# The two k weight pieces: split and stored in the first chunk instead of the second

## The chip, the cores and the metric

The kernel runs on one core of a Trainium2 chip. The metric is the device time of one execution in microseconds (us); the time of a kernel is the median of its runs. Profiles show one execution each.

## The reference

The reference is a trunk of two layers over 2560 tokens of 1024 channels: a prompt of 2048 tokens and a sample of 512, which are independent of each other. The first layer is attention in windows, with grouped heads; the second is a Fourier mixing layer. All of the change lies in the first one:

```python
def attention_layer(x, g, w_in, w_out, sink, rel_bias):
    b, s, _ = x.shape
    h = rmsnorm(x, g)
    z = h @ w_in
    q = z[..., :ATTN_WIDTH].reshape(b, s, N_HEADS, HEAD_DIM)
    k = z[..., ATTN_WIDTH:ATTN_WIDTH + KV_WIDTH].reshape(b, s, N_KV_HEADS, HEAD_DIM)
    v = z[..., ATTN_WIDTH + KV_WIDTH:ATTN_WIDTH + 2 * KV_WIDTH].reshape(b, s, N_KV_HEADS, HEAD_DIM)
    gate = z[..., ATTN_WIDTH + 2 * KV_WIDTH:]
    o = banded_gqa_with_sink(q, k, v, rel_bias, sink)
    return x + (o * jax.nn.silu(gate)) @ w_out
```

There are 16 query heads and 4 key heads of 64 channels. Each block of 128 queries sees 384 keys; the scores get a bias by relative position and the softmax has a learned sink. Everything is in 32-bit floats.

## The kernel before

**Products.** Each matrix product is made of three matmuls in a reduced 32-bit format (`fp32r`): an operand is split into a high part (its rounding, by a copy) and a low part (the rest, by a subtraction), and `matmul3` (lines 91 to 93) adds high x high, high x low and low x high. A weight piece is a tile of 128 x 1024 numbers before the split and `[128, 2, 1024]` after it: 0.5 MB raw, 1 MB split.

**Chunks.** The attention layer works through five chunks of 512 tokens: first the sample, then the four quarters of the prompt. In each chunk `make_h` brings the transposed activations (`xk`, L177), POOL scales them by the inverse norm (L179), and ACT and DVE make the high and low part of h (L183, L184; L191, L192 for the halo of 128 tokens). `kv_proj` makes k and v (`kp`, `kh`, `vp`). Then a loop of 64 steps runs over 8 pairs of heads and 8 halves of query blocks: scores (`spt`, L401), the softmax (L413 to L429), its transposes (`pt`, L440 to L442) and the product with v (`av`, L454). Between these steps TensorE is filled with the projections of the next pair's q and gate (`qp`, `gp`) and, in the last pair, with the output projection (`op`, on the pieces `wo`). Statistics of the next chunk's tokens (`xs`, L147) are spread over the steps too. Elements of `b` (L378, L382, L383) are the bias and the sink of a head.

**Weight pieces.** `load_w(c, n, ...)` (L95 to L120) delivers piece n of 28: 8 and 9 are k's, 10 and 11 are v's, 0 to 7 q's, 12 to 19 the gate's, the others the output's. In the first chunk the raw piece is loaded (`w32`, L109), ACT copies the high part (L110), and the low part is made by POOL in four quarters of 256 columns (L115) or by DVE at once (L117). The split piece is then stored in a DRAM buffer `wsd` (L119), unless n is in `AGAIN = (0, 8, 9, 10, 11, 12)`, the pieces that are wanted in the first microseconds. In the second chunk the pieces of `AGAIN` are loaded raw and split once more (ACT L101, DVE L102), and stored then by POOL's queue (L103); all others are read from `wsd` (L106), as all 28 are in the later chunks.

**Buffers and order.** Split pieces live in a ring of 4 tiles (tag `w`); raw pieces in the first chunk take tiles of two rings, `stage[0]` (tag `uT`, 8 tiles) or `stage[1]` (tag `x`, 4 tiles, which the activations, their statistics and the raw pieces of the second chunk use also). Loads are issued by SP, the stores of split pieces by POOL. A scheduler orders the instructions of each engine by the program's order and their dependencies; `after(ins, anchor)` adds a dependency of order alone: `ins` is put behind `anchor` and does not wait on its completion. `last_exp` holds the last exponential of the softmax that was issued.

Of the kernel before, what the change touches and what calls it, by code (L numbers as in the profile page):

```python
# [30 lines left out]
BIG = 1.0e30  # L31
LINE = 512
HALVES = ((1, 0), (1, 1), (0, 0), (0, 1))
AGAIN = (0, 8, 9, 10, 11, 12)
CH = 512
CHUNKS = [(2048, SEQ, T), (0, 0, SEQ), (512, 0, SEQ), (1024, 0, SEQ), (1536, 0, SEQ)]

# [1 line left out]
def f32(ap):  # L39
    return ap.bitcast(F32)  # L40
# [3 lines left out]
def encoder(  # L44
# [3 lines left out]
    PE, ACT, DVE, POOL, SP = nc.tensor, nc.scalar, nc.vector, nc.gpsimd, nc.sync  # L48
# [28 lines left out]
    def xtile(shape, dtype, name):  # L77
        return xp.tile(shape, dtype, align_bytes=LINE, tag="x", bufs=4, name=name)
# [13 lines left out]
        PE.matmul(out, a[0], b[1], start=False, stop=False, skip_group_check=more)  # L92
        PE.matmul(out, a[1], b[0], start=False, stop=stop, skip_group_check=more)  # L93

    def load_w(c, n, name, lo_engine=None):  # L95

        w = wp.tile([P, 2, D], F32R, align_bytes=LINE, tag="w", bufs=4, name=f"w{name}")
        if c == 1 and n in AGAIN:
            w32 = xtile([P, D], F32, f"w32{name}")
            SP.dma_start(w32, w_in[n])  # L100
            ACT.copy(w[:, 0], w32)  # L101
            DVE.tensor_tensor(w[:, 1], w32, f32(w[:, 0]), ALU.subtract)  # L102
            POOL.dma_start(f32(wsd[n]), f32(w))  # L103
            return w[:, 0], w[:, 1]
        if c:
            SP.dma_start(f32(w), f32(wsd[n]))  # L106
            return w[:, 0], w[:, 1]
        w32 = stage[n > 19 or n in (6, 7, 18, 19)](f"w32{name}")
        SP.dma_start(w32, w_in[n] if n < 20 else w_out[(n - 20) // 4, (n - 20) % 4])  # L109
        ACT.copy(w[:, 0], w32)  # L110
        if lo_engine is None:

            for i in range(4):
                cs = slice(i * 256, i * 256 + 256)
                POOL.tensor_tensor(w[:, 1, cs], w32[:, cs], f32(w[:, 0, cs]), ALU.subtract)  # L115
        else:
            lo_engine.tensor_tensor(w[:, 1], w32, f32(w[:, 0]), ALU.subtract)  # L117
        if n not in AGAIN:
            (SP if lo_engine else POOL).dma_start(f32(wsd[n]), f32(w))  # L119
        return w[:, 0], w[:, 1]  # L120

    stage, res_tile, ready = [], [], {}

    def after(ins, anchor):

        if anchor is not None:
            tc.add_manual_dep(ins.ins, anchor.ins.name, ISSUE, reason="issue order")

    def attention_phase():

        with ExitStack() as es:
# [6 lines left out]
            def stats(c):  # L138

                tok, lo_t, hi_t = CHUNKS[c]  # L140
                nt = min(640, hi_t - tok) // P
                ss = main.tile([P, 8], F32, tag="ss", bufs=2, name=f"ss{c}")

                def one(i):
                    xt = xtile([P, D], F32, f"xs{c}_{i}")
                    after(SP.dma_start(xt, x[tok + i * P : tok + (i + 1) * P, :]), last_exp[0])
                    sq = ACT.activation(xt, xt, AF.Square, accum_out=ss[:, i : i + 1])  # L147
                    after(sq, last_exp[0])

                return [lambda i=i: one(i) for i in range(nt)] + [lambda: inv_rms(ss, nt, f"inv{c}")]  # L150

            def spread(c, inv, place=None):

                tok, lo_t, hi_t = CHUNKS[c]
                nt = min(640, hi_t - tok) // P
                invb = ap.tile([P, 640], F32, tag="invb", name=f"invb{c}")
                for i0 in range(0, nt, 4):
                    m = min(4, nt - i0)
                    ps = bank(f"ib{c}_{i0}") if place is None else place
                    for i in range(m):  # L160
                        PE.transpose(ps[:, i * P : (i + 1) * P], inv[:, i0 + i : i0 + i + 1].to_broadcast([P, P]), ident)
                    ACT.copy(invb[:, i0 * P : (i0 + m) * P], ps[:, : m * P])  # L162
                return invb
# [40 lines left out]

            last_u = [None, None]
            early = [load_w(0, 8, "k0_0", DVE)]
            hs, halo = make_h(0, None)
            early.append(load_w(0, 9, "k0_1", DVE))

            def bias_rows():  # L210
# [27 lines left out]
            last_exp, last_evac, last_mul = [None], [None], [None]  # L238
# [7 lines left out]
            def kv_proj(c, hs, halo, norms=None, early=None):  # L246
# [9 lines left out]
                def evac_k(t, ps, n, wc):  # L256
                    ps = scaled(ps, invb, f"k{t}")
                    for j in range(2):
# [3 lines left out]
                        for rows in (slice(0, 64), slice(64, 128)):  # L262
                            ACT.copy(kw[rows, 0, cs], sp)
                            DVE.tensor_tensor(kw[rows, 1, cs], sp, f32(kw[rows, 0, cs]), ALU.subtract)

                wk = early or [load_w(c, 8 + t, f"k{c}_{t}", DVE) for t in range(2)]

                def wslice(w, k, c0, n):
# [352 lines left out]
            for c in range(len(CHUNKS)):  # L621

                if c > 1:
                    hs, halo = make_h(c, invb)
                for s in tail:
                    s()
                if c == 1:
                    hs, halo = make_h(c, invb)
                if c:
                    invb0 = kv_proj(c, hs, halo)  # L630
                else:
                    invb0 = kv_proj(c, hs, halo, first_norms, early)
                rowd, sk = bias
                uTs = []
                res = [{} for p in range(8)]
                at = [attention(c, p, res[p], uTs) for p in range(8)]
                for s in qg_proj(c, 0, hs, res[0], invb0):
                    s()
                at[0][0]()
                fill = []  # L640
                for i in range(64 + LAG + AVLAG):
                    p, n = divmod(i, 8)
                    if n == 0 and i < 64:
                        if p < 7:

                            fill = qg_proj(c, p + 1, hs, res[p + 1], invb0)
                            fill.pop(0)()
                            at[p + 1][0]()
                            if i == 0 and c == 0:

                                for s in fill[:8]:
                                    s()
                                fill = fill[8:]
                        else:
                            op = out_proj(c, uTs)
                            fill, rest, tail = op[:4], op[4:7], op[7:]
                    if c + 1 < len(CHUNKS):
                        if i == 24:
                            norm_steps = stats(c + 1)
                        if i >= 28 and i % 4 == 0 and norm_steps:  # L660
                            inv = norm_steps.pop(0)()
                        elif i == 56:
                            invb = spread(c + 1, inv)
                    if i in (4, 8, 12, 16) and c in EXTRA:
                        EXTRA[c].pop(0)()
                    if c == len(CHUNKS) - 1 and i in AHEAD:
                        AHEAD[i]()
                    if i < 64:
                        at[p][1](*HB[n])
                    k = i - LAG  # L670
                    if 0 <= k < 64:
                        at[k // 8][2](*HB[k % 8])
                    if i < 64:
                        m = len(fill) * (n + 1) // 8 - len(fill) * n // 8
                        todo = fill[len(fill) * n // 8 :][:m]
                        for s in todo[: m // 2]:
                            s()
                    k -= AVLAG
                    if 0 <= k < 64 and k % 2 == 1:
                        b = k % 8 // 2  # L680
                        at[k // 8][3](b)
                        if b % 2 == 1:
                            at[k // 8][4](b)
                    if i < 64:
                        for s in todo[m // 2 :]:
                            s()
                    elif rest:
                        rest.pop(0)()
            return tail

    def fourier_phase(tail):
        with ExitStack() as es:
# [522 lines left out]
            for i, f in enumerate(pend):  # L1215
                finish(*f, last=i == len(pend) - 1)

    fourier_phase(attention_phase())


# [96 lines left out]
```

## Time and profile before

| | |
|---|---|
| median of three runs | 1666.79 us (1666.54, 1669.78, 1666.79) |
| profiled execution | 1669.14 us |
| its span | 1667.3 us |
| mean granted TensorE clock | 0.997 |
| busy: TensorE, VectorE, ScalarE, GpSimd | 1641.9, 1173.9, 874.8, 377.7 us |
| data moved | 338.39 MB, mean 203 GB/s |

Engines are named PE (TensorE matmul), PEld (its weight loads), DVE (VectorE), ACT (ScalarE), POOL (GpSimd) and SP (SyncE); SPq and POOLq are the queues in which they issue transfers. `L101` is line 101 of the kernel. Times within a profile count from the start of its span; the execution takes 1.84 us more than its span. Of a matmul that overlaps the next one the profile models the end, so a row's length is longer than the distance to the next row. `PEclk` is the granted clock, 1.00 being full speed. What stands in brackets behind an instruction is the idle time of its engine before it and what ended it. In a row of a group, the tile left of the arrow is written and those right of it are read.

The first chunk takes from the start to about 230 us, where the second chunk's first matmul of k (`kp`) stands. The attention layer ends near 1117 us, where the Fourier layer follows.

### The profile page before, as it was taken

The page shows a single profiled execution, that of the slowest core. Times are in us where ns is not written, and L with a number is a line of the kernel's source. Part 1 is how long each engine was busy: PE and PEld are TensorE (multiplying, and loading weights), DVE is VectorE, ACT ScalarE, POOL GpSimd, SP SyncE. Part 2 cuts the span into 40 slices and gives each one's busy share as a digit, 9 for nine tenths or more (in the row PEclk, how much of TensorE's full clock was granted, in tenths as well). Part 3 has the DMA queues.
Part 4 walks back from the last instruction along what each step waited for, and adds up shares of the span by engine and source line. Part 5 has one row for each costly group of instructions (what it writes and reads, how often), then busy time and mean ns, then how long its engine had stood idle before and what let it go on. Part 6 is the DMA issues. An engine that isn't in the chain of part 4 may idle for free.

```text
span 1667.3 us, 25637 instructions
## 1 busy us (share of the span) xinstructions
PE 1641.9 (98%) x8987; PEld 1412.0 (85%) x8987; DVE 1173.9 (70%) x2812; ACT 874.8 (52%) x1998; POOL 377.7 (23%) x528
## 2 busy tenths in 40 slices
PE   9999999999999999999999999999999999999997
PEld 7888778888898888988888888888888887888886
DVE  6777665888538886478874588768576768888553
ACT  6788644676336764256652466546554545342321
POOL 2345641211403113121123211221111111111000
PEclk9999999999999999999999999999999999999999
DMA  8456886444765456754548644656456578453331
GB/s 296 167 216 224 291 318 226 181 175 175 276 222 182 158 183 211 263 200 150 199 142 327 229 166 152 231 202 246 165 196 234 183 249 316 167 187 125 113 127 51
DMA packets 89964, 338.39 MB, mean 203 GB/s; under 512 B 11067, under 2 KB 21307, under 8 KB 72684
## 3 DMA queue, kind: packets, MB, share of 16 engines
q1 hardware_dynamic: 71388, 259.40, 44.3%
q0 software_dynamic: 18160, 76.56, 11.7%
q8 instruction: 72, 1.18, 0.3%
q10 hardware_dynamic: 288, 0.79, 0.1%
q14 instruction: 56, 0.46, 0.1%
HBM read 261.18 MB, written 75.53 MB: 202 GB/s over the span
## 4 chain that ended last, share of the span: by engine, by line
PE 83%; DVE 5%; ACT 5%; DMA 4%; issue 2%; POOL 1%; SPq 0%; POOLq 0%; DVEq 0%; ACTq 0%
PE av L454 6%; PE spt L401 5%; PE pt L440 5%; PE qp L91 4%; PE qp L93 4%; PE qp L92 4%; PE gp L91 4%; PE gp L93 4%; PE gp L92 4%; PE op L91 3%; PE op L92 3%; PE op L93 3%; PE fo L92 3%; PE fo L93 3%; PE fo L91 3%; PE W L91 2%
## 5 line engine op out<-in xcount | busy, mean ns | idle before, releaser
L417 ACT ACTIVATE S<-S 128x385 f32<-128x385 f32 (+1 forms) x320 | 191.1, 597 | 44.6 <-DVE S L413 42.8
L441 ACT CAST pts<-pt 128x384 fp32r<-128x384 f32 (+1 forms) x320 | 144.2, 454 | 111.3 <-PE pt L440 106.9
L442 DVE TENSOR_TENSOR pts<-pt,pts 128x384 fp32r<-128x384 f32 (+1 forms) x320 | 168.5, 527 | 43.7 <-ACT pts L441 40.8
L413 DVE CUSTOM_DVE_ANT_0 S<-spt,b 128x385 f32<-128x385 f32 (+1 forms) x320 | 168.8, 528 | 34.6 <-PE spt L401 31.6
L401 PE MATMUL spt<-kwin,qab 128*128 128x384 f32 (+1 forms) x640 | 157.2, 327 | 1.1 <-DVE S L413 1.1
L473 POOL TENSOR_TENSOR o<-o,s 128x256 f32<-128x256 f32 x75 | 55.6, 741 | 445.0 <-DVE o L471 444.7
L440 PE MATMUL pt<-ident,S 128*128 128x128 f32 x896 | 150.6, 273 | 1.1 <-ACT S L426 0.9
L401 PEld LDWEIGHTS spt<-kwin,qab 128*128 128x128 f32 x640 | 118.2, 188 | 26.8 <-DVE S L413 1.7
L454 PEld LDWEIGHTS av<-pts,v 128*128 128x128 f32 x896 | 126.3, 189 | 14.8 <-DVE qab L350 1.6
L454 PE MATMUL av<-pts,v 128*128 128x256 f32 x896 | 136.3, 285 | 1.9 <-DVE qab L350 1.7
L91 PE MATMUL gp<-h,wg 128*128 128x512 f32 x320 | 137.8, 431 | 0.0
L91 PE MATMUL qp<-h,wq 128*128 128x512 f32 x320 | 136.8, 428 | 0.0
L91 PE MATMUL op<-wo,uT 128*128 128x512 f32 x320 | 126.5, 397 | 1.5 <-ACT invb L162 0.8
L440 PEld LDWEIGHTS pt<-ident,S 128*128 128x128 f32 x896 | 113.6, 140 | 16.0 <-DVE pts L442 3.2
L91 PE MATMUL fo<-wo,tTu 128*128 128x512 f32 x320 | 125.8, 393 | 1.3 <-ACT wo L1119 1.3
L93 PE MATMUL qp<-h,wq 128*128 128x512 f32 x320 | 126.1, 394 | 0.0
L93 PE MATMUL gp<-h,wg 128*128 128x512 f32 x320 | 125.9, 393 | 0.0
L92 PE MATMUL qp<-h,wq 128*128 128x512 f32 x320 | 125.8, 393 | 0.0
L92 PE MATMUL op<-wo,uT 128*128 128x512 f32 x320 | 125.7, 393 | 0.0
L92 PE MATMUL gp<-h,wg 128*128 128x512 f32 x320 | 125.7, 393 | 0.0
L92 PE MATMUL fo<-wo,tTu 128*128 128x512 f32 x320 | 125.4, 392 | 0.0
L93 PE MATMUL fo<-wo,tTu 128*128 128x512 f32 x320 | 124.7, 390 | 0.0
(356 smaller groups left out, 4090.2 us busy)
## 6 DMA issues: line engine op xcount, KB each, us to landing
wo<-wsd SPq DMA_DIRECT2D x32, 1024.0 KB, 5.0
wq<-wsd SPq DMA_DIRECT2D x31, 1024.0 KB, 4.8
wg<-wsd SPq DMA_DIRECT2D x31, 1024.0 KB, 6.2
x<-x1d SPq DMA_DIRECT2D x40, 512.0 KB, 3.3
b<-b21d SPq DMA_DIRECT2D x40, 512.0 KB, 5.6
b<-rowd SPq DMA_DIRECT2D x40, 384.0 KB, 4.2
xs<-in_x_dram SPq DMA_DIRECT2D x23, 512.0 KB, 6.5
s2d<-gt POOLq DMA_DIRECT2D x40, 256.0 KB, 3.5
```

The lines of the kernel that those rows point to most:

```text
L91: PE.matmul(out, a[0], b[0], start=start, stop=False, skip_group_check=more)
L92: PE.matmul(out, a[0], b[1], start=False, stop=False, skip_group_check=more)
L93: PE.matmul(out, a[1], b[0], start=False, stop=stop, skip_group_check=more)
L401: PE.matmul(ps[:, 2 + k0 * P : 2 + k1 * P], q, kwin[g][:, part, b * P + k0 * P : b * P + k1 * P], start=part == 0, stop=part == 1,)
L413: DVE.tensor_tensor_reduce(out=s[:, e0:e1], in0=ps[:, 1 + e0 : 1 + e1], in1=st["bias"][:, j, 386 - e1 : 386 - e0][:, ::-1], scale=1.0, sca ...
L417: last_exp[0] = ACT.activation(s[:, e0:e1], s[:, e0:e1], AF.Exp, bias=mn, scale=-1.0, accum_out=den)
L440: PE.transpose(ps[:, kb, :], s[:, 1 + kb * P : 1 + (kb + 1) * P], ident)
L441: ACT.copy(hi[:, k0:k1, j, :], ps[:, k0:k1, :])
L442: DVE.tensor_tensor(lo[:, k0:k1, j, :], ps[:, k0:k1, :], f32(hi[:, k0:k1, j, :]), ALU.subtract)
L454: PE.matmul(out, v, pt[:, kb].rearrange("p h q -> p (h q)"), start=kb == k0 and part == 0, stop=kb == k1 - 1 and part == 1,)
L473: eng.tensor_tensor(o, o, s, ALU.mult)
```

## The change

Pieces 8 and 9 leave `AGAIN` and form `LATE`. They are still split at the start of the first chunk as before, without a store. In the same chunk, at the fourth step of the second pair of heads (p = 1) and of the third pair (p = 2), `load_w` is called once more for one of them each: SP loads the raw piece into a tile of the `x` ring, ordered behind the last exponential; ACT copies the high part, POOL makes the low part in four quarters and stores the split piece. In the second chunk `load_w` then reads both from `wsd` as any other piece.

```diff
-AGAIN = (0, 8, 9, 10, 11, 12)
+LATE = (8, 9)
+AGAIN = (0, 10, 11, 12)
...
-    def load_w(c, n, name, lo_engine=None):
+    def load_w(c, n, name, lo_engine=None, late=None):
...
-        w32 = stage[n > 19 or n in (6, 7, 18, 19)](f"w32{name}")
-        SP.dma_start(w32, w_in[n] if n < 20 else w_out[(n - 20) // 4, (n - 20) % 4])
+        w32 = stage[late is not None or n > 19 or n in (6, 7, 18, 19)](f"w32{name}")
+        load = SP.dma_start(w32, w_in[n] if n < 20 else w_out[(n - 20) // 4, (n - 20) % 4])
+        if late:
+            after(load, late)
         ACT.copy(w[:, 0], w32)
...
-        if n not in AGAIN:
+        if late or n not in LATE + AGAIN:
             (SP if lo_engine else POOL).dma_start(f32(wsd[n]), f32(w))
         return w[:, 0], w[:, 1]
...
                     if c == len(CHUNKS) - 1 and i in AHEAD:
                         AHEAD[i]()
+                    if c == 0 and i % 8 == 3 and 1 <= p < 3:
+                        load_w(0, LATE[p - 1], f"late{p}", late=last_exp[0])
                     if i < 64:
                         at[p][1](*HB[n])
```

In the order of instructions that the scheduler makes of it, TensorE's is unchanged. On ACT, DVE, POOL and SP the order differs in the second to fourth pair of heads of the first chunk and at the start of the second chunk, and nowhere else.

## The prediction

> **What bounds the kernel now.** I read the slices of the page first, then a table of stretches, then TensorE's timeline where the change acts, then the chain of waits into it.
>
> ```profile
> PE   9999999999999999999999999999999999999997
> PEclk9999999999999999999999999999999999999999
> ```
>
> TensorE is busy nearly everywhere. So an edit can save only where TensorE stands idle, and costs only where it makes TensorE stand. The table (length, busy time and count of PE, PEld, DVE, ACT, POOL, then granted clock, DMA share, GB/s) says where that is:
>
> ```profile
> 55.00:110.00 55.00, 55.00 (x321) 48.12 (x320) 44.63 (x158) 45.35 (x113) 26.12 (x38) 1.00 0.48 175
> 110.00:180.00 70.00, 65.13 (x366) 54.80 (x365) 54.09 (x186) 59.21 (x147) 40.08 (x58) 1.00 0.70 262
> ...
> 229.00:238.00 9.00, 7.21 (x24) 5.15 (x23) 7.62 (x10) 5.09 (x6) 3.39 (x7) 0.81 0.90 320
> ...
> 262.00:1117.00 855.00, 854.48 (x4788) 744.36 (x4786) 610.75 (x1740) 464.78 (x1154) 186.99 (x243) 1.00 0.57 202
> ...
> 1383.00:1387.00 4.00, 4.00 (x18) 3.62 (x19) 2.34 (x4) 1.25 (x3) 0.00 (x0) 0.57 0.76 269
> ```
>
> Three facts: from 55 to 110 us, where two of the new splits go, PE never idles; at 229 to 238, where the second chunk's first k matmuls stand, it idles 1.8 us and has a clock of 0.81; from 262 to 1117 it idles 0.5 us in 855, so whatever is won or lost before 262 is carried on. The boundary on PE (start, length, line, idle before it in brackets):
>
> ```profile
> 213.43 0.39 PE L93 MATMUL op<-wo,uT 128*128 128x512 f32 x1
> ...
> 218.87 0.39 PE L93 MATMUL op<-wo,uT 128*128 128x512 f32 x1
> ...
> 229.75 0.39 PE L93 MATMUL op<-wo,uT 128*128 128x512 f32 x1
> 231.40 0.50 PE L91 MATMUL kp<-h,wk 128*128 128x512 f32 x1 [1.26 <-ACT wk L101]
> 231.73 0.40 PE L92 MATMUL kp<-h,wk 128*128 128x512 f32 x1
> 232.66 0.56 PE L93 MATMUL kp<-h,wk 128*128 128x512 f32 x1 [0.53 <-DVE wk L102]
> 233.02 0.63 PE L91 MATMUL kp<-h,wk 128*128 128x512 f32 x1
> ...
> 236.41 0.39 PE L93 MATMUL kp<-h,wk 128*128 128x512 f32 x1
> ```
>
> The first two rows are 24 matmuls apart: 5.44/24 = 0.227 us a matmul at full clock. The first k matmul waits for ACT's copy of the weight's high part, the third for DVE's low part. Without a wait, matmul four would start at 229.75 + 4 x 0.227 = 230.66; it starts at 233.02: **2.36 us lost**. From there eight matmuls take 236.41 - 233.02 = 3.39 us instead of 1.82: **1.57 us lost to the clock**, in this execution. The wait comes from this chain:
>
> ```profile
> 224.70 2.94 DMA xk<-in_xT_dram
> 227.80 1.57 POOL xk L179
> 229.40 0.67 ACT h L183
> 230.07 0.25 issue
> 230.32 1.04 ACT wk L101
> 231.38 1.24 DVE wk L102
> ```
>
> The last of eight activations tiles, xk_7, arrives late; ACT's and DVE's splits of k stand behind h_7 in their queues. The matmuls don't need h_7 yet: the loop over k comes first, six matmuls to each, so h_7 is first used by the 43rd.
>
> **What the change does at the boundary.** Two loads of 0.5 MB, two ACT copies, two DVE subtracts and two 1 MB stores go; two 1 MB loads of finished pieces come. In the changed program's order SP issues the first right behind xk_6 and the second right behind xk_7, where the old raw loads follow:
>
> ```profile
> 217.15 0.33 SPq L177 DMA_DIRECT2D xk<-in_xT_dram  x1
> ```
>
> ```profile
> 225.62 1.25 SPq L100 DMA_DIRECT2D w32k<-in_w_in_dram  x2
> ```
>
> The slots that they take are last read by wo's matmuls that end near 213.4 and 218.9 (the rows above), so neither issue waits for its slot. What such a load takes, from the page, and the slowest transfers of this size near that place (the two old stores):
>
> ```profile
> wq<-wsd SPq DMA_DIRECT2D x31, 1024.0 KB, 4.8
> ```
>
> ```profile
> wsd<-wk POOLq DMA_DIRECT2D x2, 1024.0 KB, 8.8
> ```
>
> Piece 8 is issued at 217.5 and lands at 222.3 to 226.3; it is needed at 229.98. Piece 9 is issued at 225.0 and lands at 229.8 to 233.8; it is needed 24 matmuls later, at 229.98 + 24 x 0.227 = 235.4. h_7, ready at 230.9, is needed at 239.5. All have slack, so I take the whole 2.36 us as won. The issue of piece 8 stands ahead of xk_7's on SP, but xk_7 waits until 224.70 for its buffer, 7 us later. Nothing of k then stands before v's splits on ACT and DVE, and the net DMA there falls by 1 MB. What could be late next is v's split, but v's matmuls come only after all of k's, 48 and then the halo's.
>
> **What it adds in the first chunk.** For each piece: a load of 0.5 MB on SP, one ACT copy, four POOL subtracts and one store issued by POOL. Rows of the same operations from 40 to 180 us (busy, mean ns, idle before):
>
> ```profile
> L110 ACT CAST wg<-w32g 128x1024 fp32r<-128x1024 f32 x6 | 6.3, 1046 | 1.7 <-PE gp L93 1.7
> ```
>
> ```profile
> L115 POOL TENSOR_TENSOR wq<-w32q,wq 128x256 fp32r<-128x256 f32 x24 | 17.1, 742 | 8.8 <-ACT wq L110 5.6 <-PE qp L93 2.5 <-PE pt L440 0.7
> ...
> L119 POOL DMA_DIRECT2D wsd<-wq x6 | 3.5, 581 | 1.5 <-POOL wq L115 1.5
> ```
>
> ACT gets 2 x 1.05 = 2.1 us. POOL gets 2 x (4 x 0.742 + 0.581 + 1.5/6) = 2 x 3.8 = 7.6 us. Between 55 and 110 ACT was busy 45.35 and POOL 26.12 of 55, so both hold it as a sum. PE's order of instructions is unchanged, so the question is order on ACT and POOL. In the new order of the second head pair, the late copy takes the place of next q's copy; q's comes behind a pts cast, g's later still:
>
> ```profile
> 73.72 0.86 ACT L441 CAST pts<-pt 128x384 fp32r<-128x384 f32 x2
> ```
>
> ```profile
> 78.28 0.39 PE L93 MATMUL qp<-h,wq 128*128 128x512 f32 x1
> ```
>
> q's copy then ends at 74.58 + 1.05 = 75.6 and its first low quarter at 76.4; the matmul at 78.28 is the first to read it: 1.8 us of slack. In the third head pair both copies (q, g) come back to back some 4 us later than now, behind the late one. ACT there:
>
> ```profile
> 85.00:90.00 5.00, 5.00 (x30) 4.33 (x29) 3.51 (x13) 4.55 (x11) 3.84 (x6) 1.00 0.02 3
> 90.00:95.00 5.00, 5.00 (x30) 4.30 (x29) 4.69 (x16) 4.29 (x11) 3.75 (x6) 1.00 0.75 316
> ```
>
> It has 0.45 + 0.71 = 1.16 us idle for 1.05 us more: it fits, with 0.1 us over. If it doesn't fit, the cost is at most the copy, 1.05. The DMA share of 0.02 and 0.75 leaves room for the transfers. On SP the first late raw load is queued behind next q's and the second ahead of it; the x buffers and w slots that they take are free by then, so nothing is held behind them, and q's copy itself comes some 4 us later in that pair, which covers a wait for half a megabyte. On POOL the stores are queued ahead of next q's quarters: their 0.581 is in the 3.8.
>
> Against that stands a stall of today whose cause is ACT's order, just after:
>
> ```profile
> 110.03 0.40 PE L93 MATMUL gp<-h,wg 128*128 128x512 f32 x1
> 111.01 0.99 PE L454 MATMUL av<-pts,v 128*128 128x256 f32 x4 [0.58 <-DVE qab L350]
> ```
>
> ```profile
> 108.38 1.06 ACT L147 ACTIVATE xs<-xs 128x1024 f32<-128x1024 f32 x1
> ...
> 109.55 0.59 ACT L349 ACTIVATE qab<-qp 64x512 fp32r<-64x512 f32 x1
> ```
>
> A square of the next chunk's activations (L147) stands before the cast and the qab that PE's av waits for. The changed order puts a cast of pts ahead of it and g's copy behind, so this stall, 0.98 - 0.23 = 0.75 us, may go. From 110 to 180 PE idles 4.9 us today in stalls that follow the same queues; they may shift by some tenths each way.
>
> **A shared port.** DVE's tiny copies of the sink beside a POOL op:
>
> ```profile
> 95.32 0.73 POOL L475 TENSOR_TENSOR uT<-o,uT 128x256 fp32r<-128x256 f32 x1 [1.25 <-ACT uT L474]
> ```
>
> ```profile
> 95.42 0.66 DVE L382 COPY b<-sk 128x2 f32<-128x2 f32 x1
> 95.99 0.16 DVE L383 COPY b<-sk 128x2 f32<-128x2 f32 x1
> ```
>
> The first copy lasts until POOL's op ends (96.05), 0.50 us longer than the second. With POOL's added quarters close by, each of the two copies can meet one, at up to 0.74 us: 0 to 1.5 us on DVE, in the second and third pair, and PE may feel it there. I take 0.75, which the 0.75 of the stall cancels. So chunk one is put at 0, between -0.75 and +2.5 (two copies at 0.74 and the 1.05 of ACT).
>
> The Trainium skill (SBUF — State Buffer, Who interferes with whom) says that DVE and GpSimd share one port pair under an exclusive lock, so that the loser blocks for the whole instruction. The trace agrees, by those 0.66 us. Taken at its worst the rule puts the sum at -0.9 in place of -2.4.
>
> **The sum.** The profiled execution took 1669.14 us (span 1667.3, 1.84 around it), 2.35 above the median 1666.79. It holds two stretches of half clock: 1.57 us here, and at 1383 to 1387 0.43 x 4.00 = 1.72 us. The median lies 2.35 below it, more than one of them and less than both, so I assume that it lacks at least this one, and leave the clock out of the forecast. Own time: 1669.14 - 2.36 - 1.57 + 0 = 1665.2. Median: 1666.79 - 2.36 + 0 = **1664.4**.
>
> **The rivals.**
>
> *The gain is larger.* The half clock sits on the k matmuls right behind the idle time; without the idle it may not come, and if the runs compared have it in the kernel before, 1.57 more goes, and the 0.75 of the stall: 1664.4 - 1.57 - 0.75 = 1662.1. For it: both windows of low clock stand where work restarts on PE, and the three runs (1666.54, 1666.79, 1669.78) lie 3.2 us apart, about two windows; and 0.9 us beyond the forecast, from any of the 4.9 us of stalls at 110 to 180, would do for a gain that can be told. Against: the median lies so low that it hardly has this window.
>
> *The weights come late: slower.* POOL's late quarters and store, 3.8 us each, stand ahead of next q's and g's. If ACT reaches q's copy more than 1.8 us later than I timed, the matmul at 78.28 waits, then likewise in the third pair, and the loss is up to 2 x 3.8 = 7.6: 1664.4 + 7.6 = 1672.0. For it: ACT's 0.1 us of slack. Against: PE doesn't idle at all there, and POOL is idle half the time.
>
> *The lock counts in full and the stall stays.* 1666.79 - 2.36 + 1.5 = 1665.9.
>
> *The read-back is late.* Landing as slowly as the two v stores in the same window (12.0 us by the DMA issues of 215 to 240), piece 9 would come at 237.0, 1.6 us late: 1666.0.
>
> ```profile
> wsd<-wv POOLq DMA_DIRECT2D x2, 1024.0 KB, 12.0
> ```
>
> **How the numbers follow.** Some 0.2% (3.3 us) is what a measurement of this kernel can tell from no change; the forecast, -2.4, lies inside. Chances: forecast 0.37, larger gain 0.34, lock 0.06, late read-back 0.06, late weights 0.17. Faster (below 1663.5) is the larger gain, 0.34; same is 0.37 + 0.06 + 0.06 = 0.49; slower (above 1670.1) 0.17. The range runs from the larger gain, less 0.3 of spread between runs, 1661.8, to the upper bound of chunk one with one window of half clock, 1664.4 + 2.5 + 1.57 = 1668.5. Of the late weights it leaves out most, and little else.
>
> **What would show it.** Right: kp follows op with no idle time before 229.98 plus shift; no L101 or L102 on wk; PE's idle in 55 to 110 at or under 0.5 us; the stall at 111 gone. The port: a sink copy of 0.5 us or more near 78 or 95, and idle before PE behind it. Wrong: idle before qp at p = 3 or 4 released by POOL wq L115, or before kp released by a DMA.

## The result and the profile after

| | before | after |
|---|---|---|
| median | 1669.15 us (1664.87 to 1671.05, 15 runs) | 1665.82 us (1662.75 to 1667.87, 15 runs) |
| ratio | | 0.9981, 95% interval 0.9973 to 0.9989 |
| profiled execution, span | 1667.3 us | 1663.8 us |

The change makes the kernel 3.2 us faster (0.19%, interval 0.11% to 0.27%). The forecast was 2.4 us. The three runs shown with the prediction lay low: over 15 runs before's median is 1669.15 us, not 1666.79.

In the changed kernel the lines stand one to three lower (L91 became L92, L101 became L102, L115 became L118, L440 became L443). The stretches of the profile after, columns as before:

```profile
55.00:110.00 55.00, 54.83 (x318) 47.64 (x317) 46.62 (x160) 46.66 (x117) 29.39 (x43) 1.00 0.61 223
110.00:180.00 70.00, 66.15 (x375) 56.12 (x374) 54.18 (x189) 60.42 (x147) 42.73 (x62) 1.00 0.74 266
...
229.00:238.00 9.00, 9.00 (x42) 7.44 (x41) 3.33 (x5) 3.12 (x4) 1.81 (x3) 1.00 0.79 307
...
262.00:1117.00 855.00, 854.25 (x4791) 744.13 (x4790) 612.28 (x1741) 465.69 (x1155) 186.74 (x243) 1.00 0.58 200
```

At 229 to 238 us PE is now busy for all 9.00 us at full clock, where it had 7.21 at 0.81. From 55 to 110 ACT has 1.3 us and POOL 3.3 us more to do, and PE loses 0.17 us. The boundary on PE:

```profile
230.51 0.39 PE L94 MATMUL op<-wo,uT 128*128 128x512 f32 x1
230.74 0.39 PE L92 MATMUL kp<-h,wk 128*128 128x512 f32 x1
230.97 0.39 PE L93 MATMUL kp<-h,wk 128*128 128x512 f32 x1
231.19 0.39 PE L94 MATMUL kp<-h,wk 128*128 128x512 f32 x1
231.42 0.39 PE L92 MATMUL kp<-h,wk 128*128 128x512 f32 x1
```

kp follows op at 0.23 us; no row has idle time in brackets. SyncE's queue and, from the view of the tile wk, what its loads took:

```profile
218.24 0.33 SPq L107 DMA_DIRECT2D wk<-wsd  x1
225.28 0.33 SPq L180 DMA_DIRECT2D xk<-in_xT_dram  x1
225.78 0.71 SPq L107 DMA_DIRECT2D wk<-wsd  x1
```

```profile
DMA to landing us min/median/max: 7.5/7.5/7.5
```

The first piece is there by about 226 us, 5 us early; the second about 233.5, and its first matmul stands 24 x 0.227 us behind 230.74, at 236.2.

At the stall of 111 us the square (L150) now stands behind the cast and the qab on ACT, and PE's av follows gp without idle time:

```profile
109.55 0.35 ACT L444 CAST pts<-pt 128x256 fp32r<-128x256 f32 x1
109.92 0.59 ACT L352 ACTIVATE qab<-qp 64x512 fp32r<-64x512 f32 x1
110.54 1.06 ACT L150 ACTIVATE xs<-xs 128x1024 f32<-128x1024 f32 x1
```

```profile
112.22 0.40 PE L94 MATMUL gp<-h,wg 128*128 128x512 f32 x1
112.45 0.64 PE L457 MATMUL av<-pts,v 128*128 128x256 f32 x4
```

PE's order is the same in both kernels, so each matmul can be compared with itself. The table below does that: the time that PE took between the same two matmuls, for every kernel of the study (one profiled execution each; the stretches are named by their times in before). "92 to 114" holds the stall at 111 us, "131 to 148" the one at 143; "wait" is the delay of the fourth k matmul against a steady 0.227 us, "clock" what the next eight lost to half clock (with the first square later the half clock begins three matmuls further on, so that the eight don't hold all of it).

| kernel | 35 to 92 | 92 to 114 | 114 to 131 | 131 to 148 | 148 to 171 | wait | clock |
|---|---|---|---|---|---|---|---|
| before | 57.62 | 21.86 | 17.02 | 17.09 | 22.89 | 2.36 | 1.57 |
| after | 57.61 | 21.14 | 17.06 | 16.74 | 22.87 | 0.00 | 0.00 |
| change again | 57.62 | 20.70 | 17.44 | 20.81 | 21.32 | 0.00 | 0.00 |
| late work alone | 57.60 | 20.72 | 17.06 | 16.76 | 22.88 | 2.20 | 0.02 |
| split first | 57.66 | 21.86 | 17.03 | 16.43 | 22.86 | 0.00 | 0.00 |
| split again | 57.68 | 21.85 | 17.30 | 20.57 | 21.35 | 0.00 | 0.00 |
| early store | 57.66 | 21.86 | 17.15 | 18.05 | 22.92 | 0.00 | 0.00 |
| first square later | 57.67 | 21.50 | 17.07 | 17.59 | 22.90 | 2.58 | 0.99 |
| piece 8 alone | 57.61 | 22.30 | 17.41 | 16.74 | 22.89 | 0.00 | 0.00 |
| piece 9 alone | 57.60 | 22.30 | 17.33 | 20.35 | 21.34 | 2.09 | 1.51 |
| sink on ACT | 57.61 | 20.70 | 17.06 | 16.72 | 22.85 | 0.00 | 0.00 |
| sink on ACT, again | 57.60 | 20.70 | 17.06 | 16.07 | 22.87 | 0.00 | 0.00 |
| split first, g later | 57.69 | 20.80 | 18.67 | 16.68 | 22.87 | 0.00 | 0.00 |
| late in pairs 5, 6 | 57.63 | 21.88 | 18.38 | 15.91 | 20.66 | 0.00 | 0.00 |

So in the two profiles the change wins 21.86 - 21.14 = 0.72 us at 111 us, 2.36 at the boundary and 1.57 of clock. That is 4.65 us, while the spans differ by 3.5: the two executions also differ where the kernels don't. By the same matching of matmuls the one of after took 1.8 us longer for the first 35 us, with half clock there, and that of before lost 1.4 us more near its half clock at 1383 us; smaller differences make up the rest.

### The profile page after: what moved, and what is told of

Its sections match the earlier page's. It is cut to its first block, busy times and chain, and to the rows that moved or that the text cites. A ratio compares the mean times of both kernels' runs of the same rounds, so it can differ in the third digit from the quotient of the medians.

```text
span 1663.8 us, 25654 instructions
## 1 busy us (share of the span) xinstructions
PE 1640.0 (99%) x8987; PEld 1410.4 (85%) x8987; DVE 1172.5 (70%) x2810; ACT 873.8 (53%) x1998; POOL 382.3 (23%) x536
## 3 DMA queue, kind: packets, MB, share of 16 engines
q8 instruction: 72, 1.18, 0.3%
## 4 chain that ended last, share of the span: by engine, by line
PE 82%; DVE 5%; ACT 5%; DMA 4%; issue 2%; POOL 1%; SPq 0%; DVEq 0%; POOLq 0%; ACTq 0%
PE spt L404 5%; PE av L457 5%; PE pt L443 5%; PE qp L92 4%; PE qp L94 4%; PE qp L93 4%; PE gp L92 4%; PE gp L94 4%; PE gp L93 4%; PE op L92 4%; PE op L94 3%; PE op L93 3%; PE fo L93 3%; PE fo L94 3%; PE fo L92 3%
## 5 line engine op out<-in xcount | busy, mean ns | idle before, releaser
L443 PE MATMUL pt<-ident,S 128*128 128x128 f32 x896 | 150.6, 273 | 0.7 <-ACT S L429 0.6
L92 PE MATMUL gp<-h,wg 128*128 128x512 f32 x320 | 137.8, 431 | 0.0
L92 PE MATMUL qp<-h,wq 128*128 128x512 f32 x320 | 136.9, 428 | 0.8 <-DVE v L318 0.8
L92 PE MATMUL op<-wo,uT 128*128 128x512 f32 x320 | 126.5, 397 | 1.5 <-ACT invb L165 0.8
L92 PE MATMUL fo<-wo,tTu 128*128 128x512 f32 x320 | 125.8, 393 | 1.3 <-ACT wo L1124 1.3
L443 PEld LDWEIGHTS pt<-ident,S 128*128 128x128 f32 x896 | 113.6, 140 | 15.7 <-DVE pts L445 3.2
```

The costliest lines, as they stand in the source:

```text
L92: PE.matmul(out, a[0], b[0], start=start, stop=False, skip_group_check=more)
L443: PE.transpose(ps[:, kb, :], s[:, 1 + kb * P : 1 + (kb + 1) * P], ident)
```

## The experiments

My theory: the wait before kp is a place in queues (the split of k behind h_7) and goes wholly; the added work of the first chunk costs nothing, and its new order on ACT takes the stall at 111 us away. The rivals: the added work costs, or the gain lies in the work that leaves the boundary.

**The late work alone.** The boundary stays as before.

```diff
-        if c == 1 and n in AGAIN:
+        if c == 1 and n in AGAIN + LATE:
```

> The late splits and stores of the first chunk stay, but the second chunk loads and splits the two k pieces once more, as before. My theory: the first chunk wins about 1 us by the changed order on ACT (the stall at 111 us gone, 1.1, that at 143 smaller, 0.3, a new one near 98, 0.45), and the wait before kp stays as it was (idle 1.3 + 0.5 us before the first and third k matmul, released by ACT and DVE splitting wk): 0.5 to 1.2 us faster than before. Rival one: the extra work of the first chunk costs time and the gain of the whole change is all at the boundary: 0 to 2 us slower than before. Rival two: the shift of the first chunk by 1 us changes what the boundary waits for, and part of the wait goes: idle before kp under 1 us.

Measured: 0.9995 (0.9985 to 1.0004), 0.8 us faster than before, not clear of nothing by the time. PE before kp:

```profile
229.73 0.50 PE L92 MATMUL kp<-h,wk 128*128 128x512 f32 x1 [1.13 <-ACT wk L102]
230.07 0.40 PE L93 MATMUL kp<-h,wk 128*128 128x512 f32 x1
230.99 0.50 PE L94 MATMUL kp<-h,wk 128*128 128x512 f32 x1 [0.52 <-DVE wk L103]
```

The wait is whole (2.20 us in the table), so rival two falls; the stretch of 92 to 114 us is 1.14 us shorter, so rival one falls. The added work isn't just free here: its order wins. In this execution no half clock followed the wait.

**The split ahead of xk_6, nothing else.**

```diff
+            early1 = []
...
                 for k in range(KD):
+                    if c == 1 and k == 6:
+                        early1.extend(load_w(1, 8 + t, f"k1_{t}", DVE) for t in range(2))
...
-                    invb0 = kv_proj(c, hs, halo)
+                    invb0 = kv_proj(c, hs, halo, None, early1 if c == 1 else None)
```

> The kernel before, with only the place of the two k pieces of the second chunk changed: they are loaded and split ahead of xk_6 and not behind xk_7; nothing is added to the first chunk. My theory: the wait before kp is a place in the queues behind h_7, not the cost of the split, so it goes wholly: kp's first matmul follows op at 0.23 us, 2.4 us faster than before (3.9 where the run of before has half a clock there). Rival: the split itself and its place in ACT's and DVE's queues cost as much elsewhere: xk_6 and xk_7 land later by two buffers of the ring, DVE's subtracts delay h_6 and h_7, and PE waits before the k matmuls that use them: less than 1 us faster, with idle on PE between 235 and 245 us released by h.

Measured: 0.9984 (0.9972 to 0.9995). On ACT, then on PE:

```profile
222.00 1.05 ACT L101 CAST wk<-w32k 128x1024 fp32r<-128x1024 f32 x1 [1.96 <-DMA w32k<-in_w_in_dram]
...
227.15 1.05 ACT L101 CAST wk<-w32k 128x1024 fp32r<-128x1024 f32 x1 [2.27 <-DMA w32k<-in_w_in_dram]
```

```profile
230.42 0.39 PE L91 MATMUL kp<-h,wk 128*128 128x512 f32 x1
230.65 0.39 PE L92 MATMUL kp<-h,wk 128*128 128x512 f32 x1
230.88 0.39 PE L93 MATMUL kp<-h,wk 128*128 128x512 f32 x1
```

The same two copies, done in the gaps of the queue, leave no wait. That shows the theory for the boundary: the price was the place, not the split. The stall at 111 stays at 0.57 us, as before.

**The early split stored at once.** The first chunk's first split of k is stored by POOL's queue, pieces 8 and 9 leave `AGAIN`, no late split.

```diff
-AGAIN = (0, 8, 9, 10, 11, 12)
+AGAIN = (0, 10, 11, 12)
...
-            (SP if lo_engine else POOL).dma_start(f32(wsd[n]), f32(w))
+            (SP if lo_engine and n not in (8, 9) else POOL).dma_start(f32(wsd[n]), f32(w))
```

> The boundary as in the change (both k pieces are read back), but the first chunk's early split is stored at once by POOL's queue, without a second split. My theory: the boundary gives 2.4 us (3.9 with the clock), and 2 MB of stores among the first loads, where the DMA engines were busy at 0.71 and PE waits for data, cost 1 to 5 us by 55 us: between 1.4 us faster and 2.6 us slower than before, with more idle on PE before 55 us than in before. Rival: the transfers of the start have room, as the share of 0.71 says, and nothing is lost: 2.4 us faster or more, so that the late split was needless.

Measured: 0.9991 (0.9982 to 1.0001). The first 35 us of this kernel, then of before:

```profile
0.00:35.00 35.00, 31.81 (x163) 24.08 (x164) 17.85 (x33) 19.98 (x29) 4.22 (x12) 0.95 0.93 340
```

```profile
0.00:35.00 35.00, 31.43 (x174) 24.61 (x175) 19.70 (x38) 22.38 (x33) 5.04 (x13) 1.00 0.83 296
```

The stores went into the room that there was: the DMA share rises from 0.83 to 0.93. PE has 11 matmuls fewer done by 35 us, but 0.05 x 35 = 1.75 us of that is half clock in this execution's first 13 us, which the profile after has too (0.95). That profile and three others with half clock there and without these stores have 162 to 168 matmuls done by 35 us, so a cost of the stores isn't seen in the 163; by the time it is inconclusive, between theory and rival.

**The first square one step later.** Only the square of ACT's at 108 us is moved.

```diff
-                        if i >= 28 and i % 4 == 0 and norm_steps:
+                        if i >= 28 and (i == 29 if c == 0 and len(norm_steps) == 6 else i % 4 == 0) and norm_steps:
```

> The kernel before, with one thing changed: the first square of the next chunk's statistics (xs, ACT) comes one step later in the loop of the first chunk, which puts the cast of pts and qab ahead of it. Theory: the stall of PE at 111 us is that square, so it goes as in the change: PE is 0.7 to 1.1 us earlier behind 112 us, and the boundary is as before: 0.5 to 1.1 us faster, hardly to be told by the time, but by the timeline. Rival: the stall went in the change because g's copy had moved off ACT there; then the square alone changes little and the stall at 111 stays over 0.4 us.

Measured: 0.9995 (0.9982 to 1.0008), nothing that can be told. The stall at 111 us shrank to 0.12 us of idle, against the rival, but the stretch won only 0.36 us of the change's 0.72 to 1.16: the square was a part of the cause. The copy of g's piece still stands ahead of the qab on ACT:

```profile
108.54 1.05 ACT L110 CAST wg<-w32g 128x1024 fp32r<-128x1024 f32 x1
...
111.47 0.59 ACT L349 ACTIVATE qab<-qp 64x512 fp32r<-64x512 f32 x1
```

The experiment "split first, and g's copy later" below puts both the copy and the square behind the qab, and there the stretch wins 1.06 us. At 143 us PE idled longer than in before, 0.99 against 0.64.

**One piece alone.**

```diff
-LATE = (8, 9)
-AGAIN = (0, 10, 11, 12)
+LATE = (8,)
+AGAIN = (0, 9, 10, 11, 12)
...
-                    if c == 0 and i % 8 == 3 and 1 <= p < 3:
+                    if c == 0 and i % 8 == 3 and 1 <= p < 2:
```

> Only piece 8 is split and stored late (in the second pair of heads) and read back; piece 9 is loaded and split in the second chunk as before. My theory: PE waits before kp for piece 8 alone, since piece 9 is first read 24 matmuls later; so all of the boundary goes: no idle on PE before the first 24 k matmuls, and none before the 25th, because ACT and DVE have piece 9 split by 233 us and it is needed at about 235. Rival: piece 9's split is then the late one, behind h_7 on both engines: idle on PE of 0.3 us or more near the 25th k matmul.

The same with 9 in place of 8:

> Only piece 9 is split and stored late (in the second pair of heads) and read back; piece 8 is loaded and split in the second chunk as before. My theory: the wait before kp stays whole, idle 1.1 to 1.3 us before the first and 0.5 us before the third k matmul, released by ACT's and DVE's split of wk: the second piece of the change buys nothing. Rival: with one split less in the queues and half a megabyte less to load ahead, piece 8 comes 0.5 us or more earlier and the idle time falls below 1.2 us in all.

One execution each (1670.38 and 1670.93 us), so only the timelines are read. Piece 8 alone leaves no idle time on PE before any k matmul, as expected. Piece 9 alone:

```profile
234.01 0.50 PE L92 MATMUL kp<-h,wk 128*128 128x512 f32 x1 [1.01 <-ACT wk L102]
234.35 0.40 PE L93 MATMUL kp<-h,wk 128*128 128x512 f32 x1
235.27 0.50 PE L94 MATMUL kp<-h,wk 128*128 128x512 f32 x1 [0.52 <-DVE wk L103]
235.61 0.55 PE L92 MATMUL kp<-h,wk 128*128 128x512 f32 x1
235.95 0.63 PE L93 MATMUL kp<-h,wk 128*128 128x512 f32 x1
```

The wait is whole and half clock follows (0.63 us a matmul). At the boundary the second late split buys nothing. But with one late piece the stretch of 92 to 114 us takes 22.30 us, 0.44 longer than before; with two it takes 20.70 to 21.14. The order of the instructions decides there, not the amount of work.

**The sink's copies on ACT.** The changed kernel, with

```diff
-                    DVE.tensor_copy(bt[:, :, 0], sk[:, 2 * p : 2 * p + 2])
+                    (ACT.copy if c == 0 and p in (3, 4) else DVE.tensor_copy)(bt[:, :, 0], sk[:, 2 * p : 2 * p + 2])
```

and the same for column 385. There are an execution by itself and a series.

> The changed kernel, with the four small copies of the sink for the fourth and fifth pair of heads done by ACT instead of DVE. Theory of the shared port: the wait of DVE on POOL's quarters there (0.67 + 0.78 and 0.43 + 0.77 us for copies that take 0.16 otherwise) goes, and with it the idle time of PE of 0.17 us near 98.8 us: PE keeps its place between 92 and 100 us against before to 0.1 us. Rival: the stall comes from ACT, which is two copies behind in that stretch; then four more copies on ACT, 0.2 us each, make it longer: 0.4 us or more lost between 92 and 100 us.

> The changed kernel with the four copies of the sink on ACT, timed. If DVE's wait on POOL's quarters costs the change what its profile showed, 0.45 us in some executions, this one is 0 to 0.5 us faster than the change and has no idle PE near 98 us. Rival: no difference that can be told, or slower because of ACT.

Measured: 0.9985 (0.9976 to 0.9994), the change beside it 0.9984 (0.9975 to 0.9993): no difference by the time. What the shared port did shows in the changed kernel's profile, DVE, POOL and PE:

```profile
96.80 0.43 DVE L385 COPY b<-sk 128x2 f32<-128x2 f32 x1
97.14 0.77 DVE L386 COPY b<-sk 128x2 f32<-128x2 f32 x1
```

```profile
95.08 2.81 POOL L118 TENSOR_TENSOR wq<-w32q,wq 128x256 fp32r<-128x256 f32 x4
97.86 0.74 POOL L118 TENSOR_TENSOR wg<-w32g,wg 128x256 fp32r<-128x256 f32 x1
```

```profile
98.83 0.85 PE L457 MATMUL av<-pts,v 128*128 128x256 f32 x5 [0.17 <-DVE pts L445]
```

The second copy ends as POOL's last quarter of wq ends, and PE waits for the cast behind it on DVE. In the kernel with the late work alone, whose order there is the same, the same copies met POOL otherwise:

```profile
94.91 0.42 DVE L385 COPY b<-sk 128x2 f32<-128x2 f32 x1
95.25 0.15 DVE L386 COPY b<-sk 128x2 f32<-128x2 f32 x1
```

No idle time followed, and the stretch took 20.72 us instead of 21.14. So the lock costs the change 0.43 us in an execution in which it strikes; in both executions with the copies on ACT it took 20.70. It struck so in one of the three profiles with the change's order of copies. In all three the copies for the pair before, near 79 us, took 0.65 to 0.67 and 0.78 us beside POOL, and PE lost nothing by it (57.60 to 57.62 us in the table).

**Split first, and g's copy later.** The second experiment, and in the first chunk:

```diff
-        ACT.copy(w[:, 0], w32)
+        after(ACT.copy(w[:, 0], w32), last_exp[0] if n == 17 else None)
```

> No late split. The second chunk's k pieces are loaded and split ahead of xk_6, and in the first chunk ACT's copy of the sixth gate piece is held until the last exponential of the fourth pair, which also puts the cast of pts ahead of the square at 111 us. Theory: the two gains of the change are both matters of order, and this has both without the added loads, copies, quarters and stores: no idle at 111 us (0.7 to 1.1 us), none before kp (2.4 us): 3.1 to 3.6 us faster than before without the clock's part, as fast as the change or up to 0.5 us faster. Rival: the gate's copy comes too late for its matmuls, or the stall moves on to 130 to 180 us; then it is as fast as with the split first alone, 2.4 to 2.7 us faster.

Measured: 0.9995 (0.9982 to 1.0008): the rival, and worse. No wait before kp, no stall at 111 us (20.80), but two new ones:

```profile
126.93 0.62 PE L458 MATMUL av<-pts,v 128*128 128x256 f32 x3 [0.45 <-DVE pts L446]
```

```profile
133.38 0.51 PE L405 MATMUL spt<-kwin,qab 128*128 128x256 f32 x2 [0.64 <-DVE S L417]
```

The stretch of 114 to 131 us takes 1.65 us more. The stall moved on.

**The change and split first again, side by side.**

> The changed kernel once more, beside the next three on one chip. Expected from the stages so far: PE idle before kp 0, stall at 111 us gone, and a time 2.4 to 4.5 us below that of before (2.4 for the wait, about 1 for the first chunk, up to 1.6 where before has half a clock behind the wait).

> The split ahead of xk_6 without late pieces, once more, beside the change itself. If the wait before kp is the main gain and only a matter of place, it is 2.0 to 3.5 us faster than before, within 1.5 us of the change. If the added work of the first chunk is what buys the time, it is under 1 us faster than before.

Measured: 0.9984 (0.9975 to 0.9993) for the change; 0.9993 (0.9984 to 1.0002) for split first. The change's gain repeats, 2.7 us. Split first gave 2.7 us in one series and 1.2 in the other, less than the 2.0 to 3.5 expected and not clear of nothing; on PE the wait was gone in both. In this series' profile of it a stall of 2.38 us stood at 146 us, with half clock behind it, and the change's has the same. The chain that ended last there, of the change again:

```profile
134.17 8.40 DMA xs<-in_x_dram
142.57 0.02 issue
142.59 1.15 ACT xs L150 x2
143.74 0.49 ACT S L420 x2
```

A load of the next chunk's activations for the statistics landed after 8.4 us, ACT's queue stood behind it, and PE behind ACT. The change itself took 16.74 us from 131 to 148 in one execution and 20.81 in the other, half clock included. That is more than the change wins.

**The late splits in the fifth and sixth pair.**

```diff
-                    if c == 0 and i % 8 == 3 and 1 <= p < 3:
-                        load_w(0, LATE[p - 1], f"late{p}", late=last_exp[0])
+                    if c == 0 and i % 8 == 3 and 4 <= p < 6:
+                        load_w(0, LATE[p - 4], f"late{p}", late=last_exp[0])
```

> The changed kernel with the late splits in the fifth and sixth pair of heads instead of the second and third; the boundary stays as in the change. There the squares of the next chunk's statistics lie on ACT as well, and the new order puts two of them ahead of a qab and a cast. Theory: the boundary gives its 2.4 us (no idle before kp), but the first chunk gives no gain and loses 1 to 3 us in stalls between 125 and 180 us, and the stall at 111 us stays at 0.58: from 1.5 us faster to 1 us slower than before. Rival: POOL and ACT have room everywhere in the first chunk, and the place makes no difference: 2.4 us faster or more.

Measured: 0.9975 (0.9964 to 0.9986), 4.2 us faster than before, the lowest median of the study (1664.35 us). The interval overlaps that of the change (0.9975 to 0.9993), so it can't be called better. My theory was right on the stalls that it named and wrong on the sum, which came out as the rival had it, though the place does make a difference:

```profile
112.22 0.99 PE L457 MATMUL av<-pts,v 128*128 128x256 f32 x4 [0.58 <-DVE qab L353]
...
131.63 0.99 PE L457 MATMUL av<-pts,v 128*128 128x256 f32 x4 [0.83 <-DVE qab L353]
150.87 0.99 PE L457 MATMUL av<-pts,v 128*128 128x256 f32 x4 [0.71 <-ACT t L465]
```

Two squares now stall PE as the first does at 111 us, but the idle times of before at 143, 151 and 170 us are gone, 1.18 us less from 131 to 148 and 2.23 from 148 to 171. Why the new order took those away wasn't tested.

## Why the prediction was right

*The boundary.* Right to the digit: 2.36 us were read as lost before the fourth k matmul, and 0.00 are lost after. Its reason, the queue behind h_7, is shown by split first, its term for piece 9 (hidden) by the two runs with one piece. The read-back took 7.5 us, between the bounds of 4.8 and 8.8; the rival of the late read-back falls.

*The clock.* The reason for leaving it out didn't hold. I took the median to lack the half clock at the boundary, because the profiled execution (1669.14 us) lay 2.35 us above the median of three runs. Over 15 runs the median is 1669.15 us, so the profiled execution is an ordinary one. Of the four profiles with the wait three have half clock right behind it, of the ten without the wait none has it there. But that its 1.57 us are won in the time isn't shown. Half clock also stands elsewhere in each of the 14 profiles (in the first 13 us, behind the stalls at 146 us, between 1380 and 1407 us), and the mean granted clock of all executions of a series is lower than before's in five of the seven series with the wait gone: 0.9964 to 0.9970 in the four series on one chip beside 0.9973 for before, 0.9971 and 0.9978 in two on another beside 0.9970, 0.9967 in one on a third beside 0.9972. One stretch of half clock is worth 3.4 x 0.5 / 1665 = 0.001. The sum below comes out without the clock, so as far as that shows leaving it out was right, by luck.

*The first chunk.* Put at 0, from -0.75 for the stall and +0.75 for the port. Measured -0.72 with the port's lock and -1.14 to -1.16 without. The mechanisms were right, two terms were mis-sized. The stall is worth 1.16, since the matmuls behind it also ran closer together: by the matched matmuls 0.75 goes at the first one and the rest at the next two. The lock costs PE 0.43, not 0.75, and in one profile of three; near 79 us it delays DVE by 1.1 us in all three, and PE by nothing. ACT's 0.1 us of slack was enough: 57.61 against 57.62 us up to 92 us, and no idle time on PE before the one at 98.83. The copies of q and g in the third pair came 6.7 and 5.4 us later against PE than in before, more than the 4 us that I read from the order, and that cost nothing either. The rival of late weights falls; no q or g matmul waited for POOL.

The rule on the shared port in the Trainium skill (SBUF — State Buffer, Who interferes with whom) agrees with the trace: the copy of 0.77 us ended as the quarter did that ended at 97.89. The worst case, 1.5 us on PE, didn't come: PE lost 0.43 us at most.

*The sum.* 2.36 and 0.72 to 1.16 make 3.1 to 3.5 us without the clock; the two series measured 3.2 and 2.7. The forecast of 2.4 lacked the stall's net: the two terms that were set against each other in the first chunk don't cancel. Its time, 1664.4 us, also started from a median that lay 2.4 us low; the two errors point opposite ways, and the measured 1665.82 lies 1.4 us above it. The prediction held 0.2% for the least that can be told from no change; with 15 runs on each side 0.19% can be (0.11% to 0.27%).

## What to carry to other kernels

Ask of a wait whether its engine was busy with the work or with the queue ahead of it: here the same split, issued ahead of two other loads, cost nothing. Price an order change on the engine by the stalls of the next stages too, and expect them to move on: three edits of the same queue won 1.1 us, won 0.4 and lost 0.4 in the same stretch. And before a median of three is taken as a base, see how far single executions lie apart.

## What was not expected of the hardware

A wait of 2.1 to 2.6 us before kp had half clock for 3.4 us behind it in three of four executions, 1.5 to 1.6 us more where the next eight matmuls hold it whole; the idle times of 2.15 to 2.62 us near 146 us had it in three of three. The same 0.5 MB load took 5.7 to 8.9 us to land within one execution (of before). The one that ACT waits for near 142 us took 6.1 us in the profile after, where PE then idled 0.30 us, and 8.4 us in the change again, where PE idled 2.62 us.
